# Strassen products for five pairs of row tiles in the second matrix of a feed-forward (Trainium2, one core)

## The chip, the cores and the metric

One core of a Trainium2 chip runs the whole program. The metric is the device time of one execution in microseconds (us), the median of several executions. A core has TensorE (PE in the profile, with its weight loads as PEld), VectorE (DVE), ScalarE (ACT), GpSimd (POOL) and SyncE (SP, here the queue that issues nearly all DMAs).

## The reference, cut to what matters

The program is an encoder trunk of two layers on 256 tokens of 1024 numbers. Each layer has two feed-forward blocks with a mixer between them, so there are four feed-forward blocks in all:

```python
def swiglu(x, w_in, w_out):
    h = x @ w_in                                  # (256,1024) @ (1024, 5632)
    gate, up = h[..., :D_FF], h[..., D_FF:]       # D_FF = 2816
    return (jax.nn.silu(gate) * up) @ w_out       # (256,2816) @ (2816,1024)

x = layer_norm(ALPHA * x + 0.5 * swiglu(x, ffn1_w_in[l], ffn1_w_out[l]), ln_g[l, 0], ln_b[l, 0])
mix = hybrid_mixer(x, ...)
x = layer_norm(ALPHA * x + mix, ln_g[l, 1], ln_b[l, 1])
x = layer_norm(ALPHA * x + 0.5 * swiglu(x, ffn2_w_in[l], ffn2_w_out[l]), ln_g[l, 2], ln_b[l, 2])
```

The change concerns the second product of `swiglu`, `(silu(gate) * up) @ w_out`.

## The kernel before, in words

All data are float32. To keep float32 accuracy on TensorE, every operand is split into a high part (a cast to float32r) and a low part (the operand minus its high part), and a product is formed as three matmuls: high by high, high by low, low by high.

**The second product.** The 2816 rows of `w_out` are 22 row tiles of 128 (JT = 22), each [128, 1024]. The gated activations are kept transposed in eleven tiles `gs[q]` of [128, 2, 2, 256]: two row tiles, high and low, 256 tokens. The function `step` (L420 to L427) multiplies row tile k for one half of the tokens (t = 0 or 1): three parts by two column halves of 512, six matmuls into two of the four PSUM accumulators `acc[t][h]`, which take four of the eight PSUM banks. The loop at L429 runs the first 15 row tiles for both token halves, twelve matmuls each. The last seven (TAIL) run for t = 0 first (L435), after which `layer_norm` (L439) of the first 128 tokens can run on VectorE while TensorE does the same seven row tiles for t = 1 (L444 to L449). In all but the last block the transposes of the normalised first half (`to_xt`, L448) stand three steps (TCUT) before the end of that.

**The weights.** `Weights._make` (L65) loads one [128, 1024] tile of weights into `raw` (5 buffers) by one DMA on SP's queue, casts it into `wh` on ScalarE (L82) and subtracts into `wl` on VectorE (L83); `wh` and `wl` have 9 buffers each. The list `srcs` holds all 316 such tiles in the order in which TensorE uses them. `get(i)` (L90) sees to it that the tiles up to i + 8 (LOOK) have been requested, so a tile is prepared up to eight tiles ahead, as soon as a buffer comes free.

**Around it.** The column steps `col` (L352) make the gated activations two columns of 128 at a time: matmuls into four PSUM banks, then for each column ScalarE copies (L382), VectorE adds (L383), a Silu (L384), a product (L386) and the split into `gs` (L388, L389). The normalisation runs on VectorE at L291, L292, L294, L296, L300 and L303, with one short step on GpSimd (L297); L280 splits transposed activations.

**Order.** TensorE's instructions run in the order in which they are written. On the other engines a planner fixes the order at build time from priorities and its own costs; weight work has its priority lowered by LATER = 100. On the chip each engine then takes its own instructions strictly in that order, and so does SP's queue of DMAs.

Of the kernel before, what the change touches and what calls it, by code (L numbers as in the profile page):

```python
# [9 lines left out]
F32 = mybir.dt.float32  # L10
F32R = mybir.dt.float32r
# [3 lines left out]
ALU = mybir.AluOpType  # L15
# [4 lines left out]
P = 128  # L20
SEQ = 256
# [3 lines left out]
JT = DFF // P  # L25
DEPTH = 2
HD = 64
ALPHA = (2.0 * DEPTH) ** 0.25
# [5 lines left out]
TAIL = 7  # L34
SPLIT = 3
TCUT = 3
LOOK = 8
NB = 4
LATER = 100
WARM = 9  # L40

# [10 lines left out]
S d 1; T sk 0; P sq 0 2; A 0 0; T sk 1; P dv 0 3; A 0 1; T sq 0; V 0; S s 0; A 1 0; S s 0; A 1 1; G; P sq 1 2; Y  # L52
0; P sq 1 1; V 1; O 0 2; T sq 1; O 0 2; B 0 0; S s 1; B 0 1; Y 1; W 0 0; W 0 1; S s 1; O 1 1; O 0 1; O 1 1; O 0
3; B 1 0; B 1 1; W 1 0; W 1 1; O 1 2; Z; O 1 4
"""


class Weights:


    def __init__(self, tc, pool, srcs):
        self.tc, self.nc, self.pool, self.srcs = tc, tc.nc, pool, srcs
        self.made = []

    def _make(self, i):  # L65
        nc = self.nc
        raw = self.pool.tile([P, 1024], F32, tag="raw", name=f"raw{i}", bufs=5)
        wh = self.pool.tile([P, 1024], F32R, tag="wh", name=f"wh{i}", bufs=9)
        wl = self.pool.tile([P, 1024], F32R, tag="wl", name=f"wl{i}", bufs=9)

        n = 512 if i < 3 else 1024
        src = self.srcs[i]

        rows = src if isinstance(src, tuple) else (src,)
        for c in range(0, 1024, n):
            s = slice(c, c + n)
            for q, r in enumerate(rows):
                h = P // len(rows)

# [8 lines left out]
            self._make(len(self.made))  # L88

    def get(self, i):  # L90
        self.upto(i + 1 + LOOK)
        return self.made[i]


# [1 line left out]
def encoder_kernel(  # L96
# [22 lines left out]
    nc = tc.nc  # L119
# [3 lines left out]
    wp = ctx.enter_context(tc.tile_pool(name="wp", bufs=1))  # L123
    gp = ctx.enter_context(tc.tile_pool(name="gp", bufs=11))
    xp = ctx.enter_context(tc.tile_pool(name="xp", bufs=5))
    tp = ctx.enter_context(tc.tile_pool(name="tp", bufs=7))
    sp = ctx.enter_context(tc.tile_pool(name="sp", bufs=4))
    ps = ctx.enter_context(tc.tile_pool(name="ps", bufs=8, space=PSUM))

    mm = nc.tensor.matmul  # L130
    dv = nc.vector


    srcs = []
    for l in range(DEPTH):
        srcs += [f1_b[l, k] for k in range(KT)]
        srcs += [f1_in[l, j, s] for j in range(JT - NB) for s in range(2)]
        srcs += [f1_out[l, k * P : (k + 1) * P, :] for k in range(JT)]
# [10 lines left out]
        srcs += [f2_out[l, k * P : (k + 1) * P, :] for k in range(JT)]  # L149
    W = Weights(tc, wp, srcs)  # L150
    wi = 0


# [155 lines left out]
    def ffn(l, n, last=False):  # L309
        nonlocal wi  # L310
        nm = f"{l}{n}"
        gs = [gp.tile([P, 2, 2, SEQ], F32R, tag="g", name=f"g_{nm}_{q}") for q in range(JT // 2)]

        def first(ts, mid=None):

            hp = [[ps.tile([P, 512], F32, tag="b", name=f"hb_{nm}_{t}{s}") for s in range(2)] for t in ts]
            for k in range(KT):
                wh, wl = W.get(wi + k)
                parts = ((0, wh, 0), (0, wl, 1), (1, wh, 2))
# [32 lines left out]
        def col(*js, flip=False):  # L352

            nonlocal wi
            ts = []
            for j in js:

                hs = [ps.tile([P, 2, SEQ], F32, tag="b", name=f"h{'gu'[s]}_{nm}_{j}") for s in range(2)]
                tl = tp.tile([P, 2, SEQ], F32, tag="tl", name=f"tl_{nm}_{j}", bufs=2)
                ws = [W.get(wi), W.get(wi + 1)]  # L360
                wi += 2
                ts.append((j, hs, tl, ws))

# [12 lines left out]
            for j, hs, tl, ws in ts:  # L376
                for s in range(2):
                    one(hs, ws, s)
            for j, hs, tl, ws in ts:
                for s in range(2):  # L380
                    two(hs, ws, s)
                    nc.scalar.copy(tl[:, s], hs[s][:, 1, :])  # L382
                    dv.tensor_tensor(tl[:, s], hs[s][:, 0, :], tl[:, s], ALU.add)  # L383
                nc.scalar.activation(tl[:, 0], tl[:, 0], AF.Silu)  # L384
                gv = tl[:, 1]
                dv.tensor_tensor(gv, tl[:, 0], gv, ALU.mult)  # L386
                q, jj = divmod(j, 2)
                nc.scalar.copy(gs[q][:, jj, 0, :], gv)  # L388
                dv.tensor_tensor(gs[q][:, jj, 1, :], gv, gs[q][:, jj, 0, :].bitcast(F32), ALU.subtract)  # L389

        first_x = l == 0 and n == 0
        if first_x:
            g0, g1 = first((0, 1))
# [4 lines left out]
        if not first_x:  # L398
            first_t(g0, 0)
        col(NB)  # L400
        if first_x:
            first_t(g0, 0)
        first_t(g1, 1)
        for j in (NB + 1, *range(NB + 2, JT, 2)):
# [5 lines left out]
            if j == JT - 6:  # L410
                gb = load_gb(l, n)
                if n == 0:
                    load_mix(l)

        acc = [[(slice(512 * h, 512 * h + 512), ps.tile([P, 512], F32, tag="b", name=f"acc_{nm}_{t}{h}"),
                 0, JT - SPLIT if last and t and h else JT) for h in range(2)] for t in range(2)]

        fin = acc[1]

        def step(k, w, t, todo):  # L420
            wh, wl = w
            q, kk = divmod(k, 2)
            gh = gs[q][:, kk, 0, t * P : (t + 1) * P]
            gl = gs[q][:, kk, 1, t * P : (t + 1) * P]
            for g, ww, e in ((gh, wh, 0), (gh, wl, 1), (gl, wh, 2)):
                for s, a, k0, k1 in todo:
                    mm(a, g, ww[:, s], start=(k == k0 and e == 0), stop=(k == k1 - 1 and e == 2))  # L427

        for k in range(JT - TAIL):  # L429
            w = W.get(wi)  # L430
            wi += 1
            for t in range(2):
                step(k, w, t, acc[t])
        ws = []
        for k in range(JT - TAIL, JT):  # L435
            ws.append(W.get(wi))
            wi += 1
            step(k, ws[-1], 0, acc[0])
        layer_norm(acc[0], 0, 0.5, gb, nm, last)  # L439
        if last:  # L440

            fin = [acc[1][0]] + [(slice(o, o + 256), ps.tile([P, 256], F32, tag="b", name=f"acc_{nm}_1{o}"),
                                  JT - SPLIT, JT) for o in (512, 768)]
        todo = [(k, acc[1]) for k in range(JT - TAIL, JT - SPLIT)]  # L444
        todo += [(k, [c]) for c in fin for k in range(JT - SPLIT, JT)]
        for i, (k, cs) in enumerate(todo):
            if i == len(todo) - TCUT and not last:
                to_xt(x[0], 0, f"y{nm}")  # L448
            step(k, ws[k - JT + TAIL], 1, cs)  # L449
            if last and cs is acc[1] and k == JT - SPLIT - 1:  # L450
# [337 lines left out]
    for l in range(DEPTH):  # L788
        ffn(l, 0)
        mixer(l)  # L790
        ffn(l, 2, last=(l == DEPTH - 1))
# [73 lines left out]
```

## Time and profile before

| | us |
|---|---|
| three runs, median | 945.54 |
| lowest and highest of them | 945.04, 945.58 |
| profiled execution, first to last instruction (its span) | 943.6 |
| TensorE busy in the span | 935.0 |
| VectorE busy in the span | 657.9 |
| ScalarE busy in the span | 524.8 |

The profile gives no device time of its own for the profiled execution: its own time is the span, and the median of the runs is 1.94 us above it. Busy time of TensorE counts each matmul from its start to a modelled end, and matmuls overlap, so that the mean of one is not the time between two. The page gives means; the timeline gives starts.

### The profile page before, as it was taken

How to read it: one execution, taken by the hardware profiler on the slowest of the kernel's cores; microseconds unless marked ns; L12 is line 12 of the kernel's file. 1: busy time of each engine (PE TensorE's matmuls, PEld its weight loads, DVE VectorE, ACT ScalarE, POOL GpSimd, SP SyncE). 2: the span in 40 equal slices, each digit the busy share in tenths (PEclk: the TensorE clock that was granted, in tenths of full speed). 3: DMA queues.
4: the chain of work that ended last, by engine and by line, in shares of the span. 5: the costliest groups of instructions: out<-in, count | busy, mean ns of one | idle time of the engine just before them, and what ended most of it. 6: DMA issues, size and time to landing. Idle time of an engine off the chain costs nothing.

```text
span 943.6 us, 13561 instructions
## 1 busy us (share of the span) xinstructions
PE 935.0 (99%) x5030; PEld 798.5 (85%) x5030; DVE 657.9 (70%) x1092; ACT 524.8 (56%) x906; POOL 17.0 (2%) x27
## 2 busy tenths in 40 slices
PE   9999999999999999999999999999999999999996
PEld 6888888888878888888889888888888889888885
DVE  7787764598987666664586666647988976666635
ACT  5777654346865666653346556543478656556520
POOL 0000000000000000000000000000000000000000
PEclk9999999999999999999999999999999999999999
DMA  9875676375426666676375666763844366666721
GB/s 325 315 265 179 192 225 192 121 240 160 129 89 211 231 179 188 193 223 198 121 249 192 196 187 194 223 190 112 279 113 134 114 234 185 187 194 190 216 66 44
DMA packets 51378, 176.28 MB, mean 187 GB/s; under 512 B 6513, under 2 KB 8305, under 8 KB 51313
## 3 DMA queue, kind: packets, MB, share of 16 engines
q1 hardware_dynamic: 51024, 175.03, 58.6%
q8 instruction: 39, 0.64, 0.3%
q10 hardware_dynamic: 288, 0.39, 0.1%
q14 instruction: 27, 0.21, 0.1%
HBM read 174.35 MB, written 1.05 MB: 186 GB/s over the span
## 4 chain that ended last, share of the span: by engine, by line
PE 98%; DVE 1%; DMA 0%; SPq 0%; issue 0%; DVEq 0%
PE acc L427 25%; PE hg L367 14%; PE hu L367 14%; PE hb L329 9%; PE hu L372 7%; PE hg L372 7%; PE ao L723 5%; PE os L659 1%; PE pj_sq L500 1%; PE pj_sq L502 1%; PE pj_dv L500 1%; PE pj_dv L502 1%; PE pj_dq L500 1%; PE pj_sq L501 1%; PE tps L617 1%; PE pj_dq L501 1%
## 5 line engine op out<-in xcount | busy, mean ns | idle before, releaser
L83 DVE TENSOR_TENSOR wl<-raw,wh 128x1024 fp32r<-128x1024 f32 (+1 forms) x319 | 384.7, 1210 | 182.9 <-ACT wh L82 108.6
L82 ACT CAST wh<-raw 128x1024 fp32r<-128x1024 f32 (+1 forms) x319 | 332.8, 1048 | 205.5 <-PE acc L427 124.4
L427 PE MATMUL acc<-wh,g 128*128 128x512 f32 (+1 forms) x710 | 191.9, 388 | 0.0
L427 PEld LDWEIGHTS acc<-wh,g 128*128 128x128 f32 x710 | 133.0, 188 | 27.1
L367 PE MATMUL hg<-xx,wh 128*128 128x512 f32 x576 | 143.2, 391 | 0.0
L367 PE MATMUL hu<-xx,wh 128*128 128x512 f32 x576 | 142.3, 389 | 0.0
L367 PEld LDWEIGHTS hu<-xx,wh 128*128 128x128 f32 x576 | 108.1, 188 | 22.5
L367 PEld LDWEIGHTS hg<-xx,wh 128*128 128x128 f32 x576 | 106.7, 188 | 21.1
L427 PE MATMUL acc<-wl,g 128*128 128x512 f32 (+1 forms) x355 | 110.9, 387 | 0.0
L372 PE MATMUL hg<-xx,wl 128*128 128x256 f32 x576 | 81.0, 283 | 0.0
L372 PE MATMUL hu<-xx,wl 128*128 128x256 f32 x576 | 80.9, 283 | 0.0
L427 PEld LDWEIGHTS acc<-wl,g 128*128 128x128 f32 x355 | 66.7, 188 | 13.6
L372 PEld LDWEIGHTS hg<-xx,wl 128*128 128x128 f32 x576 | 75.4, 191 | 1.6
L372 PEld LDWEIGHTS hu<-xx,wl 128*128 128x128 f32 x576 | 74.3, 192 | 0.0
L329 PE MATMUL hb<-wh,xx 128*128 128x512 f32 x256 | 69.4, 391 | 0.0
L382 ACT COPY tl<-hg 128x256 f32<-128x256 f32 x72 | 26.7, 370 | 58.5 <-PE hg L367 55.3
L329 PEld LDWEIGHTS hb<-wh,xx 128*128 128x128 f32 x256 | 47.7, 188 | 10.4 <-ACT wh L82 0.6
L383 DVE TENSOR_TENSOR tl<-hg,tl 128x256 f32<-128x256 f32 x72 | 30.1, 419 | 28.4 <-ACT tl L382 28.4
L388 ACT CAST g<-tl 128x256 fp32r<-128x256 f32 x72 | 29.3, 407 | 24.2 <-DVE tl L386 24.2
L329 PE MATMUL hb<-wl,xx 128*128 128x512 f32 x128 | 39.0, 391 | 0.7 <-DVE wl L83 0.7
L723 PE MATMUL ao<-wh,xx 128*128 128x512 f32 x128 | 37.0, 398 | 0.0
L382 ACT COPY tl<-hu 128x256 f32<-128x256 f32 x72 | 26.6, 369 | 18.2 <-PE hu L372 15.4
(185 smaller groups left out, 946.7 us busy)
## 6 DMA issues: line engine op xcount, KB each, us to landing
raw<-in_f_in_dram SPq DMA_DIRECT2D x144, 512.0 KB, 4.4
raw<-in_f_out_dram SPq DMA_DIRECT2D x88, 512.0 KB, 4.3
raw<-in_m_in_dram SPq DMA_DIRECT2D x36, 512.0 KB, 4.4
raw<-in_f_b_dram SPq DMA_DIRECT2D x29, 512.0 KB, 4.2
raw<-in_m_out_dram SPq DMA_DIRECT2D x8, 512.0 KB, 4.9
raw<-in_m_out_dram SPq DMA_DIRECT2D x16, 256.0 KB, 4.4
lng<-in_ln_g_dram SPq DMA_DIRECT2D x6, 512.0 KB, 4.7
lnb<-in_ln_b_dram SPq DMA_DIRECT2D x6, 512.0 KB, 5.7
```

What stands on the lines that cost most here:

```text
L82: nc.scalar.copy(wh[:, s], raw[:, s])
L83: nc.vector.tensor_tensor(wl[:, s], raw[:, s], wh[:, s].bitcast(F32), ALU.subtract)
L329: mm(hb[s], xx[:, k, g, t, :], ww[:, 512 * s : 512 * s + 512], start=(k == 0 and e == 0), stop=(k == KT - 1 and e == 2))
L367: mm(hs[s], ws[s][0][:, k * P : (k + 1) * P], xx[:, k], start=(k == 0 and not flip), stop=(k == KT - 1 and flip), skip_group_check=flip)
L372: mm(hs[s][:, 1, :], ws[s][1][:, k * P : (k + 1) * P], xx[:, k, 0], start=(k == 0 and flip), stop=(k == KT - 1 and not flip), skip_group_c ...
L382: nc.scalar.copy(tl[:, s], hs[s][:, 1, :])
L383: dv.tensor_tensor(tl[:, s], hs[s][:, 0, :], tl[:, s], ALU.add)
L388: nc.scalar.copy(gs[q][:, jj, 0, :], gv)
L427: mm(a, g, ww[:, s], start=(k == k0 and e == 0), stop=(k == k1 - 1 and e == 2))
L500: mm(o, xx[:, k, 0, t, :], wh[:, s], start=(k == 0), stop=False)
L501: mm(o, xx[:, k, 0, t, :], wl[:, s], start=False, stop=False)
L723: mm(acc[t][h], xx[:, k, g, t, :], ww[:, s], start=(k == 0 and e == 0), stop=(k == KT - 1 and e == 2))
```

## The change

In each feed-forward block ten of the 22 row tiles (those of `gs[3]` to `gs[7]`, the pairs STR) are taken in pairs. A pair has four blocks of activations, a11, a21 (first row tile, token halves 0 and 1) and a12, a22 (second row tile), and four blocks of weights, b11, b12 (first row tile, column halves) and b21, b22. The eight block products of a pair (24 matmuls with the three parts) become seven (21 matmuls), by Winograd's form of Strassen's scheme. Of the seven, three go straight into accumulators (a12 by b21, s4 by b22, a22 by t4), and four (numbers 1, 5, 6 and 7) go into four PSUM tiles of their own, `pp`, which add up over the five pairs.

The blocks' sums are made on VectorE. For the activations that is `sums`, called by `col`: four [128, 128] operations into `f`, one cast on ScalarE and one subtraction on VectorE of [128, 512]. For the weights it is `_make_pair`: two loads into `raw`, a third `raw` buffer for two sums, four [128, 512] operations, and the split into high and low parts of 3.5 tiles of [128, 1024] instead of two. A pair counts as four tiles in the look-ahead of `get`, which keeps nine in view. The order PLAN alternates single row tiles (o) and pairs (S): o o S o S o S o S S, and then come the seven row tiles of the tail as before. Behind the plan, eight VectorE operations and one ScalarE copy bring the four `pp` tiles into the residual `x`, on which the normalisation works.

The diff, cut to its core:

```diff
+STR = (3, 4, 5, 6, 7)
+PLAN = "o o S o S o S o S S"
 class Weights:
+    def _halves(self, i, raw, nm=""):
+        nc = self.nc
+        n = raw.shape[-1]
+        wh = self.pool.tile([P, 1024], F32R, tag="wh", name=f"wh{i}{nm}", bufs=9)
+        wl = self.pool.tile([P, 1024], F32R, tag="wl", name=f"wl{i}{nm}", bufs=9)
+        nc.scalar.copy(wh[:, 0:n], raw)
+        nc.vector.tensor_tensor(wl[:, 0:n], raw, wh[:, 0:n].bitcast(F32), ALU.subtract)
+        return [tuple(w[:, c : c + 512] for w in (wh, wl)) for c in range(0, n, 512)]
+
+    def _make_pair(self, i):
+        r0, r1, ta = (self.pool.tile([P, 1024], F32, tag="raw", name=f"raw{i}{c}", bufs=5) for c in "abt")
+        for r, src in zip((r0, r1), self.srcs[i][1:]):
+            nc.sync.dma_start(r, src)
+        t4 = self.tmp.tile([P, 512], F32, tag="tmp", name=f"t4_{i}")
+        a, b = slice(0, 512), slice(512, 1024)
+        with self.tc.high_priority(-LATER):
+            dv.tensor_tensor(ta[:, a], r0[:, b], r0[:, a], ALU.subtract)
+            dv.tensor_tensor(ta[:, b], r0[:, b], r1[:, b], ALU.add)
+            dv.tensor_tensor(r0[:, b], r1[:, b], ta[:, a], ALU.add)
+            dv.tensor_tensor(t4, r1[:, a], r0[:, b], ALU.subtract)
+            b21, b22 = self._halves(i, r1, "b")
+            t1, t3 = self._halves(i, ta, "t")
+            b11, t2 = self._halves(i, r0, "a")
+            (t4,) = self._halves(i, t4, "f")
+        self.made.append((b11, b21, b22, t4, t1, t2, t3))
...
     def get(self, i):
-        self.upto(i + 1 + LOOK)
+        n, live = i, 0
+        while n < len(self.srcs) and live + self._slots(n) <= LOOK + 1:
+            live += self._slots(n)
+            n += 1
+        self.upto(n)
...
                 q, jj = divmod(j, 2)
-                nc.scalar.copy(gs[q][:, jj, 0, :], gv)
-                dv.tensor_tensor(gs[q][:, jj, 1, :], gv, gs[q][:, jj, 0, :].bitcast(F32), ALU.subtract)
+                n = P if q in STR and jj == 0 else SEQ
+                nc.scalar.copy(gs[q][:, jj, 0, 0:n], gv[:, 0:n])
+                dv.tensor_tensor(gs[q][:, jj, 1, 0:n], gv[:, 0:n], gs[q][:, jj, 0, 0:n].bitcast(F32), ALU.subtract)
+                if q in STR and jj:
+                    sums(q, ts[0][2][:, 1], gv)
+        def sums(q, g0, g1):
+            f = tp.tile([P, 4, P], F32, tag="tmp", name=f"sf_{nm}_{q}")
...
+            a11, a21, a12, a22 = g0[:, 0:P], g0[:, P:SEQ], g1[:, 0:P], g1[:, P:SEQ]
+            dv.tensor_tensor(f[:, 0], a21, a22, ALU.subtract)
+            dv.tensor_tensor(f[:, 1], a11, f[:, 0], ALU.subtract)
+            dv.tensor_tensor(f[:, 2], a21, a11, ALU.subtract)
+            dv.tensor_tensor(f[:, 3], a12, f[:, 1], ALU.subtract)
+            nc.scalar.copy(sh, f)
+            dv.tensor_tensor(sl, f, sh.bitcast(F32), ALU.subtract)
+            sm[q] = sh, sl
...
-        for k in range(JT - TAIL):
+        def pair(q, w, first, final):
+            b11, b21, b22, t4, t1, t2, t3 = w
+            if first:
+                for c in (5, 7, 1, 6):
+                    pp[c] = ps.tile([P, 512], F32, tag="b", name=f"pp_{nm}_{c}")
...
+            for o, (ah, al), (bh, bl) in (
+                (acc[0][0][1], blk(1, 0), b21),
+                (acc[0][1][1], s4, b22),
+                (pp[5], s1, t1),
+                (pp[7], s3, t3),
+                (pp[1], blk(0, 0), b11),
+                (pp[6], s2, t2),
+                (acc[1][0][1], blk(1, 1), t4),
+            ):
+                own = any(o is p for p in pp.values())
+                for e, (g, ww) in enumerate(((ah, bh), (ah, bl), (al, bh))):
+                    mm(o, g, ww, start=(own and first and e == 0), stop=(own and final and e == 2))
+        for u, k in plan:
             w = W.get(wi)
             wi += 1
-            for t in range(2):
-                step(k, w, t, acc[t])
+            if u == "S":
+                pair(k, w, k == STR[0], k == STR[-1])
+            else:
+                for t in range(2):
+                    step(k, w, t, acc[t])
+        v = tp.tile([P, 512], F32, tag="tmp", name=f"v_{nm}")
+        c = 0.5 / ALPHA
+        add = lambda xs, p: dv.scalar_tensor_tensor(xs, p, c, xs, ALU.mult, ALU.add)
+        nc.scalar.copy(v, pp[1])
+        add(x[0][:, lo], pp[1])
+        dv.tensor_tensor(v, pp[6], v, ALU.add)
+        u5 = tp.tile([P, 512], F32, tag="tmp", name=f"u_{nm}")
+        dv.tensor_tensor(u5, pp[5], v, ALU.add)
+        add(x[0][:, hi], u5)
+        dv.tensor_tensor(v, pp[7], v, ALU.add)
+        add(x[1][:, lo], v)
+        dv.tensor_tensor(v, pp[5], v, ALU.add)
+        add(x[1][:, hi], v)
```

What is left out renames indices, so that the tail runs over the row tiles 5 and 16 to 21.

## Rows read from the trace of the kernel before

**Rows 1.** The page's first part (busy us and share of the span of each engine) and the row of granted TensorE clock, in tenths, over 40 slices.

```profile
PE 935.0 (99%) x5030; PEld 798.5 (85%) x5030; DVE 657.9 (70%) x1092; ACT 524.8 (56%) x906; POOL 17.0 (2%) x27
PEclk9999999999999999999999999999999999999999
```

**Rows 2.** The page's chain of work that ended last, by engine and by line.

```profile
PE 98%; DVE 1%; DMA 0%; SPq 0%; issue 0%; DVEq 0%
PE acc L427 25%; PE hg L367 14%; PE hu L367 14%; PE hb L329 9%; PE hu L372 7%; PE hg L372 7%; PE ao L723 5%; PE os L659 1%; PE pj_sq L500 1%; PE pj_sq L502 1%; PE pj_dv L500 1%; PE pj_dv L502 1%; PE pj_dq L500 1%; PE pj_sq L501 1%; PE tps L617 1%; PE pj_dq L501 1%
```

**Rows 3.** The same chain in order of time (start us, length us, what): the second products of the first, the second and the last feed-forward block.

```profile
128.38 57.80 PE acc L427 x255
...
410.28 57.80 PE acc L427 x255
...
468.95 2.08 PE acc L427 x9
...
876.46 57.81 PE acc L427 x255
```

**Rows 4.** The page's costliest groups of instructions (busy us, mean ns of one, idle time before them and what ended it): the weights' splits and the matmuls of the second products.

```profile
L83 DVE TENSOR_TENSOR wl<-raw,wh 128x1024 fp32r<-128x1024 f32 (+1 forms) x319 | 384.7, 1210 | 182.9 <-ACT wh L82 108.6
L82 ACT CAST wh<-raw 128x1024 fp32r<-128x1024 f32 (+1 forms) x319 | 332.8, 1048 | 205.5 <-PE acc L427 124.4
L427 PE MATMUL acc<-wh,g 128*128 128x512 f32 (+1 forms) x710 | 191.9, 388 | 0.0
L427 PE MATMUL acc<-wl,g 128*128 128x512 f32 (+1 forms) x355 | 110.9, 387 | 0.0
```

**Rows 5.** Timeline of TensorE (start us, us from first start to last end, what): second products, whose neighbours go to different PSUM banks, and a projection of the mixer, whose matmuls all go to one bank.

```profile
410.57 0.62 PE L427 MATMUL acc<-wl,g 128*128 128x512 f32 x2
411.02 1.07 PE L427 MATMUL acc<-wh,g 128*128 128x512 f32 x4
411.93 0.62 PE L427 MATMUL acc<-wl,g 128*128 128x512 f32 x2
...
189.65 0.39 PE L500 MATMUL pj_dq<-wh,xx 128*128 128x512 f32 x1
189.87 0.39 PE L501 MATMUL pj_dq<-wl,xx 128*128 128x512 f32 x1
```

**Rows 6.** Busy time by stretch: the last column step of the second block, the first part of its second products, the rest up to the normalisation of the first tokens, and from there to the end of the stage. Columns: stretch, its length, busy us (and instructions) of each engine, granted clock, DMA share, GB/s.

```profile
399.10:410.28 11.18, 11.18 (x66) 9.91 (x65) 8.95 (x17) 6.26 (x13) 0.00 (x0) 1.00 0.72 224
410.28:437.50 27.22, 27.22 (x121) 22.54 (x121) 14.21 (x14) 11.38 (x13) 0.00 (x0) 1.00 0.69 214
437.50:460.40 22.90, 22.90 (x102) 18.96 (x102) 7.35 (x6) 6.33 (x6) 0.00 (x0) 1.00 0.52 162
460.40:471.00 10.60, 10.60 (x52) 8.84 (x51) 10.56 (x16) 6.62 (x8) 0.92 (x1) 1.00 0.33 97
```

**Rows 7.** Timeline of VectorE around the last column step of the second block (start us, us, what, and in brackets the idle time before it and what ended that).

```profile
398.18 1.21 DVE L83 TENSOR_TENSOR wl<-raw,wh 128x1024 fp32r<-128x1024 f32 x1
...
399.64 0.41 DVE L383 TENSOR_TENSOR tl<-hg,tl 128x256 f32<-128x256 f32 x1
399.98 0.41 DVE L383 TENSOR_TENSOR tl<-hu,tl 128x256 f32<-128x256 f32 x1
...
400.98 1.22 DVE L83 TENSOR_TENSOR wl<-raw,wh 128x1024 fp32r<-128x1024 f32 x1
402.11 0.41 DVE L389 TENSOR_TENSOR g<-tl,g 128x256 fp32r<-128x256 f32 x1
402.45 1.21 DVE L83 TENSOR_TENSOR wl<-raw,wh 128x1024 fp32r<-128x1024 f32 x1
...
406.28 1.23 DVE L83 TENSOR_TENSOR wl<-raw,wh 128x1024 fp32r<-128x1024 f32 x1 [0.52 <-ACT wh L82]
```

**Rows 8.** Timeline of ScalarE in the second products.

```profile
415.75 1.05 ACT L82 CAST wh<-raw 128x1024 fp32r<-128x1024 f32 x1 [1.67 <-PE acc L427]
418.47 1.05 ACT L82 CAST wh<-raw 128x1024 fp32r<-128x1024 f32 x1 [1.67 <-PE acc L427]
```

**Rows 9.** Timeline of VectorE at the end of the second products, and TensorE's transposes of the first normalised tokens there.

```profile
452.20 1.23 DVE L83 TENSOR_TENSOR wl<-raw,wh 128x1024 fp32r<-128x1024 f32 x1 [1.49 <-ACT wh L82]
460.41 1.29 DVE L291 SCALAR_TENSOR_TENSOR x<-acc,x 128x512 f32<-128x512 f32 x2 [6.98 <-PE acc L427]
...
465.61 1.41 DVE L303 SCALAR_TENSOR_TENSOR x<-x,rs,lnb 128x512 f32<-128x512 f32 x2
...
467.92 1.03 PE L275 MATMUL tr_y<-ident,x 128*128 128x128 f32 x8
...
469.81 0.68 DVE L280 TENSOR_TENSOR xx<-tr_y,xx 128x512 fp32r<-128x512 f32 x1
470.40 0.68 DVE L292 BATCH_NORM_STATS2 st<-x 128x6 f32<-128x512 f32 x1
```

**Rows 10.** The page's DMA issues: size of one and median us from issue to landing.

```profile
raw<-in_f_out_dram SPq DMA_DIRECT2D x88, 512.0 KB, 4.3
```

**Rows 11.** Timeline of VectorE at the end of the kernel, where the second operation reads what the first has written.

```profile
936.45 0.42 DVE L291 SCALAR_TENSOR_TENSOR x<-acc,x 128x256 f32<-128x256 f32 x1
936.90 0.43 DVE L292 BATCH_NORM_STATS2 st<-x 128x6 f32<-128x256 f32 x1
```

More of the change, by code (lines that the diff above doesn't have):

```diff
@@ L58, with __init__, _slots @@
 class Weights:
-    def __init__(self, tc, pool, srcs):
-        self.tc, self.nc, self.pool, self.srcs = tc, tc.nc, pool, srcs
+    def __init__(self, tc, pool, tmp, srcs):
+        self.tc, self.nc, self.pool, self.tmp, self.srcs = tc, tc.nc, pool, tmp, srcs
         self.made = []
+    def _halves(self, i, raw, nm=""):
[7 more added lines that the diff above has]
+    def _make_pair(self, i):
+        nc, dv = self.nc, self.nc.vector
+        r0, r1, ta = (self.pool.tile([P, 1024], F32, tag="raw", name=f"raw{i}{c}", bufs=5) for c in "abt")
[13 more added lines that the diff above has]
+        self.made.append((b11, b21, b22, t4, t1, t2, t3))
+    def _slots(self, i):
+        return 4 if self.srcs[i][0] == "S" else 1
     def _make(self, i):
         nc = self.nc
+        if self.srcs[i][0] == "S":
+            return self._make_pair(i)
         raw = self.pool.tile([P, 1024], F32, tag="raw", name=f"raw{i}", bufs=5)
@@ L131, in encoder_kernel, with out_rows @@
     dv = nc.vector
+    singles = [k for k in range(JT) if k // 2 not in STR]
+    singles, tail = singles[: len(singles) - TAIL], singles[len(singles) - TAIL :]
+    plan, left, pairs = [], list(singles), list(STR)
+    for u in PLAN.split():
+        plan.append((u, (left if u == "o" else pairs).pop(0)))
+    assert not left and not pairs
+    def out_rows(w):
+        row = lambda k: w[k * P : (k + 1) * P, :]
+        rows = [row(k) if u == "o" else ("S", row(2 * k), row(2 * k + 1)) for u, k in plan]
+        return rows + [row(k) for k in tail]
     srcs = []
@@ L137, in encoder_kernel @@
         srcs += [f1_in[l, j, s] for j in range(JT - NB) for s in range(2)]
-        srcs += [f1_out[l, k * P : (k + 1) * P, :] for k in range(JT)]
+        srcs += out_rows(f1_out[l])
         for c in range(3):
@@ L148, in encoder_kernel @@
         srcs += [f2_in[l, j, s] for j in range(JT - NB) for s in range(2)]
-        srcs += [f2_out[l, k * P : (k + 1) * P, :] for k in range(JT)]
-    W = Weights(tc, wp, srcs)
+        srcs += out_rows(f2_out[l])
+    W = Weights(tc, wp, tp, srcs)
     wi = 0
@@ L387, in col @@
                 q, jj = divmod(j, 2)
-                nc.scalar.copy(gs[q][:, jj, 0, :], gv)
-                dv.tensor_tensor(gs[q][:, jj, 1, :], gv, gs[q][:, jj, 0, :].bitcast(F32), ALU.subtract)
+                n = P if q in STR and jj == 0 else SEQ
[3 more added lines that the diff above has]
+                    sums(q, ts[0][2][:, 1], gv)
+        sm = {}
+        def sums(q, g0, g1):
+            f = tp.tile([P, 4, P], F32, tag="tmp", name=f"sf_{nm}_{q}")
+            if STR.index(q) < 3:
+                s = xp.tile([P, 2, 4, P], F32R, tag="x", name=f"s_{nm}_{q}")
+                sh, sl = s[:, 0], s[:, 1]
+            else:
+                sh, sl = (tp.tile([P, 4, P], F32R, tag="tmp", name=f"s{c}_{nm}_{q}") for c in "hl")
+            a11, a21, a12, a22 = g0[:, 0:P], g0[:, P:SEQ], g1[:, 0:P], g1[:, P:SEQ]
[6 more added lines that the diff above has]
+            sm[q] = sh, sl
         first_x = l == 0 and n == 0
@@ L413, in ffn @@
                     load_mix(l)
+        k0, k1 = singles[0], tail[-1]
+        kl = tail[-SPLIT]
         acc = [[(slice(512 * h, 512 * h + 512), ps.tile([P, 512], F32, tag="b", name=f"acc_{nm}_{t}{h}"),
-                 0, JT - SPLIT if last and t and h else JT) for h in range(2)] for t in range(2)]
+                 k0, tail[-SPLIT - 1] if last and t and h else k1) for h in range(2)] for t in range(2)]
         fin = acc[1]
@@ L425, in step @@
             for g, ww, e in ((gh, wh, 0), (gh, wl, 1), (gl, wh, 2)):
-                for s, a, k0, k1 in todo:
-                    mm(a, g, ww[:, s], start=(k == k0 and e == 0), stop=(k == k1 - 1 and e == 2))
-        for k in range(JT - TAIL):
+                for s, a, ka, kb in todo:
+                    mm(a, g, ww[:, s], start=(k == ka and e == 0), stop=(k == kb and e == 2))
+        pp = {}
+        def pair(q, w, first, final):
[3 more added lines that the diff above has]
+                    pp[c] = ps.tile([P, 512], F32, tag="b", name=f"pp_{nm}_{c}")
+            sh, sl = sm[q]
+            blk = lambda kk, t: [gs[q][:, kk, e, t * P : (t + 1) * P] for e in range(2)]
+            smb = lambda c: (sh[:, c], sl[:, c])
+            s1, s2, s3, s4 = (smb(c) for c in range(4))
+            for o, (ah, al), (bh, bl) in (
[10 more added lines that the diff above has]
+                    mm(o, g, ww, start=(own and first and e == 0), stop=(own and final and e == 2))
@@ L430, in ffn @@
+        for u, k in plan:
             w = W.get(wi)
             wi += 1
-            for t in range(2):
-                step(k, w, t, acc[t])
+            if u == "S":
+                pair(k, w, k == STR[0], k == STR[-1])
+            else:
+                for t in range(2):
+                    step(k, w, t, acc[t])
+        v = tp.tile([P, 512], F32, tag="tmp", name=f"v_{nm}")
+        c = 0.5 / ALPHA
+        lo, hi = slice(0, 512), slice(512, 1024)
+        add = lambda xs, p: dv.scalar_tensor_tensor(xs, p, c, xs, ALU.mult, ALU.add)
@@ L434, in ffn @@
+        nc.scalar.copy(v, pp[1])
[8 more added lines that the diff above has]
+        add(x[1][:, hi], v)
         ws = []
-        for k in range(JT - TAIL, JT):
+        for k in tail:
             ws.append(W.get(wi))
@@ L442, in ffn @@
             fin = [acc[1][0]] + [(slice(o, o + 256), ps.tile([P, 256], F32, tag="b", name=f"acc_{nm}_1{o}"),
[L443 to L447, printed above, removed]
+                                  kl, k1) for o in (512, 768)]
+        todo = [(i, acc[1]) for i in range(TAIL - SPLIT)]
+        todo += [(i, [c]) for c in fin for i in range(TAIL - SPLIT, TAIL)]
+        for n_, (i, cs) in enumerate(todo):
+            if n_ == len(todo) - TCUT and not last:
                 to_xt(x[0], 0, f"y{nm}")
-            step(k, ws[k - JT + TAIL], 1, cs)
-            if last and cs is acc[1] and k == JT - SPLIT - 1:
+            step(tail[i], ws[i], 1, cs)
+            if last and cs is acc[1] and i == TAIL - SPLIT - 1:
                 s, a = acc[1][1][:2]
```

## The prediction, made before the changed kernel was run

> **What bounds the kernel now.** I read the engines' totals first. TensorE is busy for 935.0 of the 943.6 us of the span and its granted clock is full in all forty slices [rows 1]; VectorE has 70%, ScalarE 56%. The chain of waits says the same from the end backwards: 98% of the time is TensorE's and a quarter of the chain is line L427, the second products [rows 2]. The chain in order of time shows that this quarter is four unbroken stretches, one to a feed-forward block: 255 matmuls in 57.80 us, then the transposes and nine more [rows 3]. So every matmul taken out of L427 should shorten the program, unless TensorE then waits for the engines that prepare its operands.
>
> The price of a matmul must be read with care. The groups give 388 ns as the mean of one [rows 4], but matmuls overlap. The stretch gives 57.80 / 255 = 0.2267 us from start to start, and the timeline agrees: four matmuls from 411.02, the next at 411.93 [rows 3, 5]. By the mean of 388 ns one would expect 60 x 0.388 = 23.3 us of gain; by the starts it is 13.6. I take the starts, because TensorE's end is set by them.
>
> **What the change removes.** 24 matmuls of a pair become 21, of the same width: 3 x 5 pairs x 4 blocks = 60 matmuls of 512 columns, 60 x 0.2267 = 13.60 us. In a pair three matmuls in a row go to one PSUM bank, where before the neighbours alternated; a projection with all its matmuls in one bank starts them 0.22 to 0.23 us apart too [rows 5], so that costs nothing. Loads of TensorE stay one per matmul.
>
> The Trainium skill ("TensorE: Matmul & The Clock Gate", Part 1, the part on the 56 ns) puts back-to-back matmuls of 512 columns 215.7 ns apart at full clock; the sum would be 12.9 us by it. The rows here show 226.7 ns, and the measurement decides.
>
> **What it adds on VectorE.** Prices again from start to start. A [128, 1024] split takes 402.11 - 400.98 = 1.13 us, a 256-column operation 0.335 us (399.64 to 399.98) [rows 7], a 512-column one 0.60 us (469.81 to 470.40) [rows 9]. No row has a 128-column sum of two tensors in SBUF: it can't be below the constant that the 256 and 1024 rows leave, 0.07 us, nor above the 0.335 us of 256 columns; I take the line between them, 0.20. An operation that reads what the one before it wrote starts 0.45 us after a 256-column one instead of 0.335 [rows 11], so I add 0.11 for each such step.
> - Weights of a pair: four sums, two of them dependent, 4 x 0.60 + 0.22 = 2.6 us, and 3.5 splits, 3 x 1.13 + 0.60 = 4.0: 6.6 us instead of 2.26, so 4.35 more.
> - Activations of a pair: 4 x 0.20 + 0.60 and some dependence, less half a split of 256 columns: 1.6 us (between 1.1 and 2.2 by the bounds).
> - Closing of a block: eight operations of 0.60 + 0.11: 5.7 us.
>
> That is 5 x (4.35 + 1.6) + 5.7 = 35.5 us in a block, 142 in all: VectorE goes from 658 to about 800 of 930 us. ScalarE gets 1.5 casts more for a pair (mean 1.05 [rows 4]) and a half for its activations, some 45 us in all, to 570. Neither total is the bound. DMA bytes are the same.
>
> **Whether it stays hidden, stage by stage.** In the column steps there is room: the last one has 8.95 us of VectorE's 17 operations in 11.18 [rows 6], by starts about 7.5, and a column step with a pair's activations adds 1.6. No matmul waits for them soon, since the first pair comes after the last column step.
>
> In the second products I count from T, their start (410.28). A single tile is 12 matmuls, 2.72 us; a pair 4.76; a step of the tail 1.36. So TensorE reaches the five pairs at T + 5.4, 12.9, 20.4, 27.9 and 32.6, the tail at 37.4, and ends the first token half at 46.9. A pair and a single take TensorE 7.48 us and VectorE 6.6 + 1.13 = 7.73; the last two pairs stand together, 4.76 against 6.6. So here VectorE is as slow as TensorE, and what counts is its lead at T. Before, the splits of the second to fifth tile of the look-ahead ran at T - 12.1, - 9.3, - 7.8 and - 4.0 [rows 7], as buffers came free; these four buffers are now the first pair's. Its four sums are 2.6 us less the 0.5 us by which its last split is shorter, and the last column step has 11.18 - 7.5 = 3.7 us of room. So the first pair is ready at about T - 2, 7 us before its use.
>
> From T to T + 46.9 VectorE has the rest of the last column (1.5), three singles (3.4), four pairs (26.4), seven tail splits (7.9) and the closing (5.7): 44.9 us in 46.9. Before, in the same part of the stage (the second and third stretch), it had 21.6 us of 50.1 [rows 6], and its engines waited for TensorE to free buffers: the casts start 2.72 us apart, each 1.67 us idle [rows 8]. This idle time is the cover of the change, and nearly all of it is used up; 2.0 us are left, and the two us ahead of T.
>
> What is late next, if it is not enough: the tail's own splits, and then the normalisation of the first tokens. That starts when the first half is done, has VectorE to itself (10.56 of 10.60 us busy [rows 6]), and ends at 467.02; its transposes start on TensorE at 467.92 [rows 9]. So it may come 0.9 us late for nothing, and more is paid by TensorE in three blocks of four (the last has no such transposes).
>
> Buffers: nine `wh` and `wl` hold two pairs and a single, so a pair's last split waits until the single before the preceding pair's end is used, some 7 us ahead of need. Of five `raw` buffers a pair holds three, so the second load of the next pair goes out when the split that frees a buffer is done (3.7 us into a pair's preparation) and lands 4.3 us later [rows 10]: at 8.0, where the next pair's second sum wants it at 6.6 + 1.1 + 0.6 = 8.3. That fits, if a freed buffer goes to whoever is next. SP's queue takes its DMAs in order, and behind a load that waits there are only loads of later tiles. PSUM: four `pp` tiles and four accumulators fill the eight banks; the four that the last column step leaves are free by T + 2, the first pair comes at T + 5.4. The closing frees them before the transposes.
>
> So the sum: 945.54 - 13.60 = **931.9**; for the profiled execution 943.6 - 13.6 = 930.0 of span, if what lies around it stays at 1.9. I predict 932.0 us.
>
> **The rivals.**
> - *VectorE sets the pace.* If its operations cost their full durations (0.68 for 512 columns [rows 9], 1.22 for 1024 [rows 7]) and not the starts, the same list is 4 x 7.1 + 3 x 1.22 + 1.7 + 7 x 1.22 + 6 = 48.2 us in 46.9: 1.3 us late in a block, 5 us in all, **937**. For it: the splits and sums wait for ScalarE and for each other more than the back-to-back rows do. Against: rows 7 show that neighbours overlap by 0.08 us. The Trainium skill ("VectorE: DVE Perf Modes", The DRAIN you can't avoid) says that the next operation can't start until the pipe is empty; by that rule this rival would be the forecast.
> - *The gain is used up.* If `raw` buffers are handed out in strict turn, the next pair's second load waits for the pair's third split, not the first. From split to split of that place it is then 4.3 + 2.0 + 3.4 = 9.7 us instead of 7.7. Starting from T - 2.6 the fifth pair has that split at T + 36.2 and VectorE ends its list at 36.8 + 13.6 = 50.4, 3.5 us late: four times that is the gain, **946**, no change. Nothing in this trace tells how buffers are handed out, since before each tile took one.
> - *Slower.* VectorE's order is fixed at build time, so one operation of the first pair whose load or buffer is late holds all behind it. With the same strict turn, and the first pair's preparation 4 us later than T - 2, the list ends 7.5 us late: 30 us in all, **962**. It decides above 3.4 us lost in a block (13.6 / 4). For it: the pair's three `raw` buffers are more than half of the five. Against: before, the loads had landed long before the splits, which waited for TensorE instead [rows 4].
>
> **Chances.** Forecast (931 to 935, nothing or up to 0.9 us lost in a block) 0.65; VectorE's pace (935 to 943) 0.20; used up 0.05; slower 0.10. A measurement of this kernel can tell about 0.2%, 1.9 us, from no change. Faster by more than that is then 0.85, within it 0.05, slower 0.10. The forecast's own range is 931 to 935. For 8 in 10 I reach into the second case: 930.8 to 941; below the lower end nothing reaches, since 60 starts are all that goes.
>
> **What the profile of after would show.** Right: 4970 matmuls instead of 5030, TensorE with no idle time in the second products, each such stage 3.4 us shorter (its first stretch and the transposes), VectorE's busy sum near 800 us and over nine tenths busy in these stages, its splits still waiting for ScalarE or TensorE now and then. Wrong: a row of waits in which TensorE waits for VectorE at the pairs (the pace), at the tail's splits or at the transposes (the lead), or VectorE waiting for a DMA ahead of a pair's sums (the `raw` buffers). The prediction fails above all if VectorE has more than 2 us of idle time between T and T + 46.9 that no buffer of TensorE's forces.

## The result, and the profile after

| | before | after |
|---|---|---|
| median of the runs, us | 945.45 | 931.88 |
| lowest and highest | 945.04, 945.58 | 931.21, 932.27 |
| span of the profiled execution, us | 943.6 | 930.1 |

The ratio is 0.9858, with a 95% interval of 0.9844 to 0.9872: 13.6 us faster. The forecast was 932.0. One of the ten executions of a later experiment, the one with more work in the closing, took 1328.43 us at a mean granted clock of 0.653 and is left out of that experiment's figures.

The engines' totals, the granted clock, the chain by engine, and the splits' group, of the page of the changed kernel (beside [rows 1, 2, 4]):

```profile
span 930.1 us, 13767 instructions
PE 922.0 (99%) x4970; PEld 788.2 (85%) x4970; DVE 789.5 (85%) x1344; ACT 569.1 (61%) x970; POOL 17.0 (2%) x27
PEclk9999999999999999999999999999999999999998
PE 99%; DVE 1%; issue 0%; DVEq 0%
L119 DVE TENSOR_TENSOR wl<-raw,wh 128x1024 fp32r<-128x1024 f32 (+1 forms) x279 | 336.1, 1210 | 73.7 <-PE hg L424 28.8
```

TensorE has 60 matmuls fewer and 13.0 us less of busy time. VectorE has 132 us more. Idle time in front of the single tiles' splits has fallen from 183 us to 74 (the pairs' splits stand in groups of their own), and the largest part of it now waits for the column matmuls, not for ScalarE's casts as before [rows 4]. In the whole run TensorE waits for no operand; this is all that the list of its waits holds, at the very start:

```profile
PE wps L217 <- PEq L971: 0.8, 1, 0.8
```

The chain in order of time through the second products of the second block (start us, length us, what), and below it, from TensorE's timeline, the transposes behind them (beside [rows 3, 9]):

```profile
406.83 5.44 PE acc L503 x24
...
440.83 2.72 PE pp L527 x12
444.23 17.00 PE acc L503 x75
```

```profile
461.07 1.03 PE L327 MATMUL tr_y<-ident,x 128*128 128x128 f32 x8
```

From the first matmul to the transposes it is 461.07 - 406.83 = 54.24 us, before 467.92 - 410.28 = 57.64: 3.40 us in a block, 15 matmuls of 0.2267 us, and four blocks make the 13.6.

VectorE in the last column step and from the start T of the second products (406.83) to the end of the first token half (stretch, length, busy us and instructions by engine, clock, DMA share, GB/s; beside [rows 6]). VectorE is the third engine of a row. Busy time counts overlapping operations once: 209 matmuls of some 0.39 us each make 46.87 us busy in a stretch of 46.87. So VectorE is idle for 46.87 - 43.11 = 3.8 us of the second stretch.

```profile
395.60:406.83 11.23, 11.23 (x66) 9.96 (x66) 11.10 (x21) 6.20 (x13) 0.00 (x0) 1.00 0.41 131
406.83:453.70 46.87, 46.87 (x209) 38.81 (x208) 43.11 (x51) 26.57 (x30) 0.00 (x0) 1.00 0.72 236
```

Its timeline (start us, us, what, idle before): the last pieces of the first pair, a split of the second pair, the waits for a load, the last piece of the fifth pair, the end of the closing and the normalisation.

```profile
398.94 1.22 DVE L73 TENSOR_TENSOR wl133a<-raw133a,wh133a 128x1024 fp32r<-128x1024 f32 x1
...
402.41 0.69 DVE L73 TENSOR_TENSOR wl133f<-t,wh133f 128x512 fp32r<-128x512 f32 x1
403.01 0.68 DVE L89 TENSOR_TENSOR t<-raw135b,raw135a 128x512 f32<-128x512 f32 x1
...
406.46 1.23 DVE L73 TENSOR_TENSOR wl135b<-raw135b,wh135b 128x1024 fp32r<-128x1024 f32 x1
...
412.24 0.69 DVE L87 TENSOR_TENSOR raw137t<-raw137a,raw137b 128x512 f32<-128x512 f32 x1 [0.33 <-DMA raw137b<-in_f_out_dram]
412.96 0.69 DVE L88 TENSOR_TENSOR raw137a<-raw137b,raw137t 128x512 f32<-128x512 f32 x1
...
421.68 0.69 DVE L87 TENSOR_TENSOR raw139t<-raw139a,raw139b 128x512 f32<-128x512 f32 x1 [0.50 <-DMA raw139b<-in_f_out_dram]
...
434.70 0.68 DVE L73 TENSOR_TENSOR wl140f<-t,wh140f 128x512 fp32r<-128x512 f32 x1
...
452.90 0.69 DVE L540 SCALAR_TENSOR_TENSOR x<-v,x 128x512 f32<-128x512 f32 x1
453.56 1.29 DVE L343 SCALAR_TENSOR_TENSOR x<-acc,x 128x512 f32<-128x512 f32 x2
...
458.77 1.41 DVE L355 SCALAR_TENSOR_TENSOR x<-x,rs,lnb 128x512 f32<-128x512 f32 x2
```

Tile number 133 is the first pair, 135, 137, 139 and 140 are the next four. The first pair is ready at T - 3.7, all four sums of the second at T - 3.1, the fifth pair at T + 28.6, eight us before TensorE wants its last product (T + 36.7). The closing ends where the normalisation starts, and that ends 0.9 us before its transposes, as in the kernel before (458.77 + 1.41 = 460.18 against 461.07).

### The profile page after: what moved, and what is told of

It is laid out like the page before. It is cut to its first block, busy times and chain, and to the rows that moved or that the text cites. A ratio compares the mean times of both kernels' runs of the same rounds, so it can differ in the third digit from the quotient of the medians.

```text
span 930.1 us, 13767 instructions
## 1 busy us (share of the span) xinstructions
PE 922.0 (99%) x4970; PEld 788.2 (85%) x4970; DVE 789.5 (85%) x1344; ACT 569.1 (61%) x970; POOL 17.0 (2%) x27
## 4 chain that ended last, share of the span: by engine, by line
PE 99%; DVE 1%; issue 0%; DVEq 0%
PE hg L419 14%; PE hu L419 14%; PE acc L503 14%; PE hb L381 9%; PE hu L424 7%; PE hg L424 7%; PE pp L527 6%; PE ao L840 5%; PE acc L527 4%; PE os L776 1%; PE pj_sq L619 1%; PE pj_sq L617 1%; PE pj_dv L617 1%; PE pj_sq L618 1%; PE pj_dq L617 1%; PE pj_dv L619 1%
## 5 line engine op out<-in xcount | busy, mean ns | idle before, releaser
L119 DVE TENSOR_TENSOR wl<-raw,wh 128x1024 fp32r<-128x1024 f32 (+1 forms) x279 | 336.1, 1210 | 73.7 <-PE hg L424 28.8
L118 ACT CAST wh<-raw 128x1024 fp32r<-128x1024 f32 (+1 forms) x279 | 290.6, 1047 | 117.4 <-PE acc L503 29.3
L503 PE MATMUL acc<-wh,g 128*128 128x512 f32 (+1 forms) x390 | 109.0, 387 | 0.0
L503 PEld LDWEIGHTS acc<-wh,g 128*128 128x128 f32 x390 | 72.9, 188 | 14.7
L503 PE MATMUL acc<-wl,g 128*128 128x512 f32 (+1 forms) x195 | 61.6, 386 | 0.0
L503 PEld LDWEIGHTS acc<-wl,g 128*128 128x128 f32 x195 | 36.6, 188 | 7.3
L434 ACT COPY tl<-hu 128x256 f32<-128x256 f32 x72 | 26.8, 372 | 20.2 <-PE hu L424 17.1
L441 ACT CAST g<-tl 128x128 fp32r<-128x128 f32 (+1 forms) x72 | 27.1, 376 | 15.9 <-DVE tl L438 14.0
L436 ACT ACTIVATE tl<-tl 128x256 f32<-128x256 f32 x72 | 30.2, 419 | 6.5 <-DVE tl L435 5.6
```

The costliest lines, as they stand in the source:

```text
L441: nc.scalar.copy(gs[q][:, jj, 0, 0:n], gv[:, 0:n])
L503: mm(a, g, ww[:, s], start=(k == ka and e == 0), stop=(k == kb and e == 2))
```

## The experiments

**An eighth product put back.** TensorE does 24 matmuls to a pair again, VectorE all of the change's work.

```diff
                 (acc[1][0][1], blk(1, 1), t4),
+                (acc[1][1][1], blk(1, 1), b22),
             ):
```

> The changed kernel with an eighth block product in each pair (three more matmuls, into the accumulator acc[1][1], so that the second products are no longer the reference's): 24 matmuls to a pair as before the change, and all of the change's work on VectorE. Theory (the matmuls taken out are the whole gain, at 0.2267 us from start to start): 60 matmuls back, 931.9 + 13.6 = 945.5 us. Rival (a part of the gain came from other waits or from a shorter path into the normalisation): clearly below 945, by the part that came from elsewhere; 940 would mean 5 us.

Measured: 945.06 us; the kernel before, on the same chip, 945.10; ratio 0.9999 (0.9989 to 1.0008). Its page has all the added work of VectorE and the old count of matmuls:

```profile
PE 935.1 (99%) x5030; PEld 798.4 (85%) x5030; DVE 789.4 (84%) x1344; ACT 567.3 (60%) x970; POOL 17.0 (2%) x27
```

So the 60 matmuls are the whole gain: 945.06 - 931.88 = 13.2 us, 0.22 each (13.4 us against the 931.64 of the next experiment, on the same chip). 388 ns each, the mean of the groups, would have made it 23.

**The sums left out.** 21 matmuls to a pair, VectorE's work as before the change. The third `raw` buffer of a pair goes as well.

```diff
-            dv.tensor_tensor(ta[:, a], r0[:, b], r0[:, a], ALU.subtract)
-            dv.tensor_tensor(ta[:, b], r0[:, b], r1[:, b], ALU.add)
-            dv.tensor_tensor(r0[:, b], r1[:, b], ta[:, a], ALU.add)
-            dv.tensor_tensor(t4, r1[:, a], r0[:, b], ALU.subtract)
             b21, b22 = self._halves(i, r1, "b")
-            t1, t3 = self._halves(i, ta, "t")
             b11, t2 = self._halves(i, r0, "a")
-            (t4,) = self._halves(i, t4, "f")
+            t1, t3, t4 = b22, b21, t2
...
-                if q in STR and jj:
-                    sums(q, ts[0][2][:, 1], gv)
...
-        nc.scalar.copy(v, pp[1])
-        add(x[0][:, lo], pp[1])
...
```

> The changed kernel with 21 matmuls to a pair, but without the sums of weights and activations and without the closing (products of plain blocks, the four pp tiles never read, so that the second products are left incomplete): VectorE does what it did before the change. Theory (all the added work on VectorE, 130 us of busy time, lies beside the matmuls): the same as the changed kernel, 931.9 us within 0.5. Rival (VectorE costs TensorE something somewhere): faster than 931.9, by what it costs; 928 would mean 1 us in each block.

Measured: 931.64 us (931.50 to 931.85), against 931.88 (931.21 to 932.27): the same.

```profile
PE 922.0 (99%) x4970; PEld 788.1 (85%) x4970; DVE 658.5 (71%) x1092; ACT 524.7 (56%) x906; POOL 17.0 (2%) x27
```

131 us of VectorE's busy time and 44 of ScalarE's cost nothing here. That they are hidden does not say how close they are to showing; the next three runs do.

**More work in each pair: two, four and six operations of 512 columns.**

```diff
+            for _ in range(2):     # 4 and 6 in the others
+                dv.tensor_tensor(t4, r1[:, a], r0[:, a], ALU.subtract)
             dv.tensor_tensor(t4, r1[:, a], r0[:, b], ALU.subtract)
```

> The changed kernel with two further operations of 512 columns in the preparation of each pair of weights (t4 written twice more before its real value; the result is the reference's). They are 1.2 us more for a pair, 6.0 in a block. From the start of the second products to the end of the first token half VectorE of the changed kernel is busy for 43.1 of 46.9 us by the profile, by starts for some 38.7, so it has about 8 us of idle time. Theory (that idle time can be used): hidden, 932 to 933. Rival (the prediction's own count, 2.0 us left in a block): 2.8 to 4.0 us late in a block, 943 to 948 in all.

> Four further operations of 512 columns in the preparation of each pair of weights (two were hidden, six cost 50 us): 2.4 to 2.8 us for a pair, 12 to 14 in a block, of which a fifth falls ahead of the second products. Theory (some 8 us of idle time in a block, of which part is forced by buffers that TensorE has yet to free): 1.5 to 3.2 us late in a block, 938 to 945 us, and some us more where TensorE's clock falls after a wait. Rival (the room ends right behind two operations, and what comes later is paid in full): 6 to 8 us late in a block, 956 to 964 us. Rival (the cost of six came mainly from order and clock, and four are still hidden): 932 to 933 us.

> The same with six further operations for a pair: 3.6 to 4.2 us for a pair, 18 to 21 in a block, of which the first pair's fall ahead of the second products. Theory (some 8 us of idle time in a block, and 2 in the last column step): 8 to 11 us late in a block, four blocks, 964 to 976. Rival (2.0 us left): 12 to 16 late in a block, 980 to 996. TensorE should then wait for VectorE at the pairs and at the tail's first tiles.

Measured: 932.05 us with two, 952.13 with four, 982.30 with six. Two are hidden: the theory, not the 2.0 us of the prediction. Four cost 20.2 us, 5.1 in a block, between what theory and rival gave. By starts (0.60 us) they are 5 x 4 x 0.60 = 12.0 us in a block, so about 7 us of work found room, and two operations (6.0 us) were just inside it. With six, 18.0 - 7 = 11 us in a block would be 44 in all; measured are 50.4; the wait of 3.8 us below and the section on the hardware return to the difference.

The 8 us of idle time in the expectations are not what the row shows: they take the overlaps off a busy time that counts them once already, and 3.8 us are idle. VectorE's total has risen by less than the starts say, too (first two operations, then four, against 789.5):

```profile
PE 921.9 (99%) x4970; PEld 787.7 (85%) x4970; DVE 806.4 (87%) x1384; ACT 568.1 (61%) x970; POOL 17.0 (2%) x27
PE 932.4 (98%) x4970; PEld 785.1 (83%) x4970; DVE 830.9 (87%) x1424; ACT 565.9 (60%) x970; POOL 17.0 (2%) x27
```

16.9 us for 40 operations are 4.2 in a block, not 6.0; 41.4 for 80 are 10.4, not 12.0. One reason stands in the timeline: an operation that needs the one before it starts 0.72 us after it (412.24 to 412.96), and one more put between the two fills a part of that. In busy time the room is then about 10.4 - 5.1 = 5 us in a block. The changed kernel has 3.8 us idle behind T and some more ahead of it; how much of the added work each took was not worked out.

Where four show: the first two of TensorE's waits (total, times, longest), and below them the timelines of VectorE and of TensorE in the tail of the second block.

```profile
PE acc L505 <- DVE wl L121: 6.6, 12, 0.7
PE pj_dk L620 <- DVE wl L121: 1.3, 2, 0.7
```

```profile
452.08 1.22 DVE L121 TENSOR_TENSOR wl<-raw,wh 128x1024 fp32r<-128x1024 f32 x1
453.21 0.68 DVE L547 TENSOR_TENSOR u<-pp,v 128x512 f32<-128x512 f32 x1
453.81 1.22 DVE L121 TENSOR_TENSOR wl<-raw,wh 128x1024 fp32r<-128x1024 f32 x1
```

```profile
453.35 0.73 PE L505 MATMUL acc<-wl,g 128*128 128x512 f32 x2 [0.67 <-DVE wl L121]
...
455.09 0.73 PE L505 MATMUL acc<-wl,g 128*128 128x512 f32 x2
```

No wait at a pair is longer than 0.2 us. But the fifth pair is ready only at T + 36.8 (T is 412.64 here), the tail's splits have no lead left, and the planner has put one or two operations of the closing between them. With one, a tail tile takes VectorE 453.81 - 452.08 = 1.73 us, where TensorE takes 1.36: TensorE goes at VectorE's pace (455.09 - 453.35 = 1.74). The listed waits, 6.6 us, are less than the 20 lost, because the matmuls behind a short wait are counted busy to their modelled ends (TensorE's busy time is 932.4 us instead of 922.0). The second line is the mixer, where matmuls of a projection wait for splits, twice in the whole run.

Where six show, in the same list: the pairs themselves are late too.

```profile
PE tr_y L329 <- DVE x L357: 5.1, 6, 1.5
PE acc L529 <- ACT wh140f L72: 3.8, 1, 3.8
...
PE acc L529 <- DVE wl140b L73: 1.4, 1, 1.4
```

The wait of 3.8 us, for ScalarE's cast of the fifth pair's last sum, comes once in each block, 15 us in all. VectorE makes that sum at L91, and in its fixed order operations of the closing stand ahead of it, the first of which waits 1.02 us:

```profile
460.84 0.69 DVE L542 SCALAR_TENSOR_TENSOR x<-pp,x 128x512 f32<-128x512 f32 x1 [1.02 <-ACT v L543]
...
463.25 0.68 DVE L91 TENSOR_TENSOR t<-raw140b,raw140a 128x512 f32<-128x512 f32 x1
```

**More work in the closing.**

```diff
         dv.tensor_tensor(v, pp[6], v, ALU.add)
+        for _ in range(8):
+            dv.tensor_tensor(v, pp[6], v, ALU.add)
```

> The changed kernel with eight further operations of 512 columns in the closing, each reading what the one before wrote, ahead of the second half of the first tokens' residual (they add a PSUM tile again, so that the second products are not the reference's): 8 x 0.71 = 5.7 us more in front of the first normalisation of each block. In the changed kernel the closing ends at 453.58, where the normalisation begins at 453.56, and the transposes that wait for it begin 0.9 us after its end. Theory A (order can give way: two splits of the next stage and the four operations for the second tokens, 5.1 us, go behind the normalisation): 932 to 934 us. Theory B (the order stays): 4.8 us late in each of the three blocks with transposes, 931.9 + 14.4 = 946 us, with TensorE waiting at the transposes for VectorE.

Measured: 949.0 us, the median of nine executions (944.9 to 952.2; ratio to before 1.0040, 1.0026 to 1.0054), theory B and 3.0 us more. The profiled one of them took 950.63. In the second products TensorE waits three times, in the three blocks with transposes:

```profile
PE tr_y L327 <- DVE x L355: 11.8, 3, 4.3
```

VectorE's timeline in the second block:

```profile
461.44 0.68 DVE L343 SCALAR_TENSOR_TENSOR x<-acc,x 128x512 f32<-128x512 f32 x1
...
466.22 0.68 DVE L551 TENSOR_TENSOR v<-pp,v 128x512 f32<-128x512 f32 x1
...
470.60 1.41 DVE L355 SCALAR_TENSOR_TENSOR x<-x,rs,lnb 128x512 f32<-128x512 f32 x2
```

The operations for the second tokens did not go behind the normalisation but into it (466.22), so that it takes 10.6 us from 461.44 instead of 6.6. Counted from T (412.92 here), it ends 5.7 us later than without the added work (59.1 against 53.4), and the transposes start 4.2 us later (58.5 against 54.2). So about 1.5 us were free in front of them, somewhat more than the 0.9 us between the normalisation's end and the transposes: they start here (471.40) when the first of its two last operations, which end at 472.01, is done.

**A sixth pair, and the changed kernel beside it.** The room of 7 us by starts asks for the next 5.9.

```diff
-STR = (3, 4, 5, 6, 7)
-PLAN = "o o S o S o S o S S"
+STR = (3, 4, 5, 6, 7, 8)
+PLAN = "o S o S o S S S S"
```

> The changed kernel with a sixth pair (the row tiles of gs[8]; the plan is o S o S o S S S S, the tail stays at seven): three matmuls fewer in each block, 4 x 3 x 0.2267 = 2.72 us, and 6.6 - 2.26 + 1.6 = 5.9 us more on VectorE in each block, of about 8 us that the changed kernel leaves idle. The activations' sums of three pairs now hold six of the seven tmp buffers. Theory (the idle time can be used, as two more operations for each pair could): 929.2 us. Rival (four pairs in a row take VectorE 26.4 us beside 19.0 us of matmuls, or the one free tmp buffer holds up the sums): 1 to 5 us late in a block, 933 to 949 us, with TensorE waiting for VectorE at the fifth and sixth pair.

> The changed kernel itself beside the two others on one chip, for a direct comparison: 931.9 us within 0.5.

Measured: 928.99 us (928.44 to 929.36) with six pairs, 931.88 (931.58 to 932.13) with five: 2.89 us, where twelve matmuls by 0.2267 make 2.72. The ratio to the kernel before is 0.9828 (0.9813 to 0.9843). No wait of TensorE in the stage is listed, and VectorE is busy for 44.5 of 46.2 us. Its total is 803.8 us, 3.6 us in a block more than with five pairs, where 5.9 were expected. The stretch from the start of the second products to the end of the first token half, and below it the timeline of VectorE at the end of the closing:

```profile
405.55:451.74 46.19, 46.19 (x205) 38.24 (x205) 44.51 (x55) 28.01 (x32) 0.00 (x0) 1.00 0.65 218
```

```profile
452.74 1.28 DVE L343 SCALAR_TENSOR_TENSOR x<-acc,x 128x512 f32<-128x512 f32 x2
453.94 1.28 DVE L344 BATCH_NORM_STATS2 st<-x 128x6 f32<-128x512 f32 x2
455.13 0.68 DVE L540 SCALAR_TENSOR_TENSOR x<-v,x 128x512 f32<-128x512 f32 x1
```

Here one operation of the closing (455.13) did go behind the start of the normalisation. This version beats both kernels. In front of the transposes hardly any margin is left in this block: the last operation of the normalisation ends at 459.73, and the second four transposes start at 459.78 (the first line is VectorE's timeline, the others are TensorE's chain).

```profile
458.31 1.42 DVE L355 SCALAR_TENSOR_TENSOR x<-x,rs,lnb 128x512 f32<-128x512 f32 x2
459.27 0.51 PE tr_y L327 x4
...
459.78 0.66 PE tr_y L327 x4
```

## Why the prediction was right, step by step

- *The price of a matmul from start to start.* Right, and it decided the forecast: 13.6 us predicted, 13.6 measured, and 13.2 came back with the eighth product.
- *Nothing for three matmuls in a row into one bank.* Right: twelve matmuls into the `pp` tiles take 2.72 us, 0.2267 each.
- *What it adds on VectorE.* About 142 us of operations counted by starts, measured 131.6 of busy time; ScalarE some 45, measured 44. The items are of the right size, a little dear.
- *VectorE's list between T and T + 46.9.* Wrong in size, on the safe side: 44.9 us forecast, 43.1 measured, and in these are two splits for the next stage (nine splits of single tiles run behind the fifth pair, where the tail needs seven), 2.3 us that the list did not have. So 40.8 us of the list's work fell there. The step that failed is the lead. The prediction had the first pair ready at about T - 2 and the second wholly behind T. In fact the last column step was filled to 11.10 of 11.23 us, the first pair was ready at T - 3.7, and the second pair's four sums, a single and a part of a split (2.6 + 1.1 + 0.4 us) were done before T as well; that is the difference. So 2.0 us were forecast as left, 3.8 are idle in the row, and the runs with more work in each pair show room for about 5 us of busy time, 7 by starts. The prediction's own sign of being wrong was more than 2 us of idle time there that no buffer of TensorE's forces. Of the 3.8 us, some 2.2 stand in front of operations that a load held up, directly or through ScalarE's cast; what held those loads was not followed up, so this stays open.
- *The room in the last column step.* Misread: 8.95 us of busy time [rows 6] were cut to 7.5 for overlaps that a busy time counts once already. The row leaves 11.18 - 8.95 = 2.2 us, not 3.7. The lead was larger all the same, because the first pair's sums ran before that step.
- *The `raw` buffers.* Right: the second load of the third pair goes out at 407.72, as soon as the second pair's first split (406.46 + 1.2) frees a buffer, and not after its third (410.68 + 1.2), and VectorE waits for a load 0.33 and 0.50 us in this block. Buffers are handed to whoever is next here; the two rivals that rested on a strict turn fall with that. The load in the timeline of SP's queue:

```profile
407.72 0.33 SPq L82 DMA_DIRECT2D raw137b<-in_f_out_dram  x1
```

- *VectorE sets the pace.* No: rows of after start 0.60 to 0.61 us apart for 512 columns (402.41 to 403.01), not 0.68. The prediction took from the Trainium skill ("VectorE: DVE Perf Modes", The DRAIN you can't avoid) that the next operation can't start until the pipe is empty; the same section adds that one which is not held starts earlier, and these rows agree with that. Neighbours without a dependence overlap here. As a mechanism this rival is real, though: with four more operations in a pair it is what TensorE's tail shows.
- *What is late next.* Right in kind and place: the tail's splits first (four operations more), the normalisation's transposes when the closing grows. The free time in front of the transposes was put at 0.9 us; the run with more work in the closing shows about 1.5.

The time would have been the same had the room been the 2.0 us of the prediction. So the result alone did not test that step; the added work did.

## What to carry to other kernels

Price a removed matmul by the time from start to start in the stretch, not by the mean of its group; here the two differ by a factor of 1.7. Work that is hidden has a room that the result does not show: count it at the place where the other engine's lead is smallest, with the work that was done ahead of the stage, and measure it by adding known amounts until they show. Busy time counts an overlap once, so take none off a second time. Where room is left, as 5 to 7 us here, the next step of the same trade (a sixth pair, 2.9 us) can be had for it.

## What the runs showed of the hardware that was not expected

A wait of TensorE can cost more than itself, because the clock can fall behind it. With eight operations more in the closing, TensorE's transposes waited 4.08 us and then ran at half pace; with six more in each pair, waits of 0.57 and 1.37 us in a row were followed by matmuls 0.43 us apart instead of 0.23. In both stretches the granted clock is 0.50, the lower of its two levels (1.2 GHz). First the transposes and the row of their stretch, then a wait, starts and the row from the other kernel (columns as in [rows 6]):

```profile
471.40 1.97 PE L327 MATMUL tr_y<-ident,x 128*128 128x128 f32 x8 [4.08 <-DVE x L355]
471.45:473.40 1.95, 1.95 (x9) 1.95 (x10) 1.95 (x3) 0.59 (x1) 0.00 (x0) 0.50 0.00 0
```

```profile
455.07 0.80 PE L529 MATMUL acc<-wl140b,g 128*128 128x512 f32 x1 [1.37 <-DVE wl140b L73]
...
456.09 0.63 PE L529 MATMUL acc<-wh140b,sh 128*128 128x512 f32 x1
456.52 0.63 PE L529 MATMUL acc<-wl140b,sh 128*128 128x512 f32 x1
```

```profile
455.10:458.40 3.30, 3.30 (x8) 2.62 (x9) 3.30 (x4) 0.00 (x0) 0.00 (x0) 0.50 0.21 60
```

In the undisturbed kernel the eight transposes take 1.03 us from the first start to the last end, here 1.97. Transposes and the nine matmuls behind them take 476.00 - 471.40 = 4.60 us instead of 464.02 - 461.07 = 2.95. With the transposes 4.2 us late that is 5.9 in this block; all three blocks together make most of the 18.8 us by which the profiled execution of the closing's run is longer (950.63 against 931.88). With six operations more in each pair the mean granted clock was 0.984, with four, where no wait is longer than 0.7 us, it stayed full (0.999). TensorE's busy time does not tell the two apart: it grew to 932.4 us with four and to 942.2 with six. How much of the 6 us by which the six-operation run is above its 44 is the clock, and how much the wait of 3.8 us that VectorE's order makes in each block, was not separated.
